# Column-wise substitution in the 16x16 blocks, and key products kept without their strengths, in a hybrid DeltaNet layer

## The chip, the cores and the metric

The kernel runs on one core of one Trainium2 chip. The metric is the device time of one execution in microseconds (us), lower is better. The engines are named as in the profile: PE (TensorE, with PEld for its weight loads), DVE (VectorE), ACT (ScalarE), POOL (GpSimd) and SP (SyncE, which here only starts transfers).

## The reference, cut to what matters

One layer works on 2048 latent tokens and 256 context tokens of width 1024. Branch A is a gated delta rule with 8 heads of 128 columns, run in both directions over chunks; the output of both directions is added, normalised, gated and projected. The part that the change touches is the inside of one chunk:

```python
m = jnp.where(tri_strict, jnp.einsum('bhncd,bhnsd->bhncs', k_beta, k) * decay, 0.0)
t_inv = lax.linalg.triangular_solve(eye + m, jnp.broadcast_to(eye, m.shape), left_side=True, lower=True)
u = jnp.einsum('bhncs,bhnsv->bhncv', t_inv, v_beta)
w = jnp.einsum('bhncs,bhnsd->bhncd', t_inv, k_beta * jnp.exp(g_cum)[..., None])
qk = jnp.einsum('bhncd,bhnsd->bhncs', q, k) * decay
def step(s, xs):
    v_new = u_i - jnp.einsum('bhck,bhkv->bhcv', w_i, s)
    o = jnp.einsum('bhck,bhkv->bhcv', q_dec_i, s) + jnp.einsum('bhcs,bhsv->bhcv', qk_i, v_new)
    s = s * d_i[..., None, None] + jnp.einsum('bhck,bhcv->bhkv', k_dec_i, v_new)
```

So each chunk needs the products of its keys with its keys (and with its queries), scaled by a decay and by a strength per key, and the inverse of a triangular matrix made from the first. The result need not be computed in chunks of 64; the kernel takes chunks of 128.

## The kernel before, in words

The kernel has three stages. The first computes the input projections (to about 1.85 ms of the trace). The second, called the window here, runs the delta rule. The third is the output projection with the final normalisation.

The window is a list of 36 **visits**: 18 chunks of 128 tokens (two of the context, sixteen of the latent tokens), each visited once in each direction, the two directions taking turns. A loop over i works on four visits at a time: v0 = visit i is in its state update (`st_ks`, `st_v`, `st_o`, `st_u`), v1 in the later steps of its inverse (`inv_w16` to `inv_d64`), v2 in its query products (`gram` with QK), v3 in its loads, its decays (`visit_decay`), its key products (`gram` with N) and the inverse of its 16x16 blocks (`inv_base`). Between them the loop puts a fixed number of **fillers**, single 512-column matmuls of the other projections (L1249, L1251, L1253), 24 a visit while i is under 25. PE's instructions run in the order in which the loop writes them. The order on DVE, ACT, POOL and SP is fixed when the kernel is built, by a scheduler; each of these engines then takes its list strictly in order.

A chunk is met twice, once in each direction. At the first meeting (a **fresh** visit; 16 of the 32 latent visits, all of them ahead of the others) `gram` computes the key products and stores them in DRAM (`kkd`, `kqd`) for the other direction. At the second meeting (an **again** visit) it loads them and multiplies them by that direction's decay (L151, L152).

The steps of a visit that the texts below speak of, with their lines in the kernel before:

- L137: ACT makes exp(gcb) for the queries (`qd`); POOL multiplies it by the queries (L138). DVE may overwrite `gcb` only after L137.
- L140: DVE, 8 times, difference of cumulated decays, with the mask. L142: ACT, exp of the result, so `gcb` now holds the decays of all 8 heads.
- L158: PE, key products, into two PSUM banks of 4 heads each. L163: ACT copies a bank to `zat`. L164: POOL multiplies the copy by the other direction's strengths. L165: SP stores it.
- L167: DVE, one instruction a head, products times strength (`cj`) times decay, gives N (and QK).
- L177, L180, L181, L182: ACT, then DVE, cut the 16x16 diagonal blocks out of N into `n16`.
- L191 to L193: the loop of 15 steps that inverts the blocks: a shuffle that spreads one row of R over its block, a multiplication, an addition. R is 128 x 8 heads x 16 columns.
- L196, L198: ACT spreads R to `r32`, DVE transposes it. L210 to L226: the step from 16 to 32. L247 to L267: from 32 to 64, ending in `r64t`.
- L278: PE, first product of the last step, needs `r64t`. L281: ACT copies it to `w64`. L288: PE, second product. L289: ACT puts it in R.
- L300, L302: PE and DVE, state times keys. L309, L312: new values and their copy. L320, L321: outputs. L328, L333: state update. L1287, L1288: ACT copies the output of a fresh visit, SP stores it.
- L118: POOL scales the keys of a later update (`kt`).

Of the kernel before, what the change touches and what calls it, by code (L numbers as in the profile page):

```python
# [7 lines left out]
F32 = mybir.dt.float32  # L8
# [24 lines left out]
def bc(ap, n):  # L33

    return ap.to_broadcast([ap.shape[0], ap.shape[1], n])


class Kern:
# [81 lines left out]
    def visit_decay(self, v):  # L120
# [21 lines left out]
        nc.scalar.activation(out=gcb, in_=gcb, func=AF.Exp)  # L142
        v["cj"] = cj

    def gram(self, v, name, rhs):
# [8 lines left out]
        for g in range(2):  # L154
# [4 lines left out]
            if v["latent"]:  # L159

                kc = self.g1.tile([P, 4, P], F32, name="zat", bufs=2)
                co = self.cc[:, v["n"], 8 - 8 * v["d"]:16 - 8 * v["d"]]
                nc.scalar.copy(out=kc, in_=kk)  # L163
                nc.gpsimd.tensor_tensor(out=kc, in0=kc, in1=bc(co[:, hs].unsqueeze(2), P), op=ALU.mult)  # L164
                nc.sync.dma_start(keep[:, hs], kc)  # L165
            for h in range(4 * g, 4 * g + 4):
                nc.vector.scalar_tensor_tensor(out=N[:, h, :], in0=kk[:, h - 4 * g, :], scalar=v["cj"][:, h:h + 1],  # L167
                                               in1=v["gcb"][:, h, :], op0=ALU.mult, op1=ALU.mult)


    def inv_base(self, v):
# [13 lines left out]
        nc.gpsimd.tensor_copy(out=R, in_=rows(self.i16))  # L185
        rb = g2.tile([P, H, 16], F32, name="rb")
        for i in (range(15, 0, -1) if d == 0 else range(0, 15)):
            c0, c1 = (i, 16) if d == 0 else (0, i + 1)
            w = c1 - c0
            rbv = rb.rearrange("p h c -> p (h c)")[:, 0:H * w].rearrange("p (h c) -> p h c", c=w)  # L190
            nc.vector.stream_shuffle(rbv, R[:, :, c0:c1], [i] * 16 + [16 + i] * 16)  # L191
            nc.vector.tensor_tensor(out=rbv, in0=rbv, in1=bc(n16[:, :, i:i + 1], w), op=ALU.mult)  # L192
            nc.vector.tensor_tensor(out=R[:, :, c0:c1], in0=R[:, :, c0:c1], in1=rbv, op=ALU.add)  # L193
        v["r32"] = r32 = g2.tile([P, H, 32], F32, name="r32")
# [974 lines left out]
    def window(self, es, settle):  # L1169
# [105 lines left out]
        def o_cb(n, again):  # L1275
# [7 lines left out]
            def cb(g, po):  # L1283
                hs = slice(4 * g, 4 * g + 4)
                ot = self.g1.tile([P, 4, P], F32, name="ot", bufs=3)
                if not again:
                    nc.scalar.copy(out=ot, in_=po)  # L1287
                    nc.sync.dma_start(self.o_d[n][:, hs], ot)  # L1288
                else:
                    nc.vector.tensor_tensor(out=ot, in0=po, in1=op[g], op=ALU.add)  # L1290
                    late.append((n, hs, ot))
# [354 lines left out]
```

## Time and profile before

| | us |
|---|---|
| median of 3 runs | 3217.88 |
| lowest and highest | 3211.53 and 3222.15 |
| the profiled execution | 3213.67 |
| its span in the trace | 3211.9 |
| granted PE clock, mean over the span | 0.965 of full speed |

The profiled execution is one run with a trace; its own time is 1.8 us more than the span that the trace covers, and it lies 4.2 us below the median of the three runs. All sums below are made against it. The trace has a row for each instruction with its start and its duration; neighbouring instructions of one engine overlap a little, so the distance from start to start is what an instruction costs its engine when nothing holds it up.

### The profile page before, as it was taken

What the parts mean: (1) busy time and instruction counts of PE and PEld (TensorE: products, weight loads), DVE (VectorE), ACT (ScalarE), POOL (GpSimd) and SP (SyncE); (2) the same over time, 40 slices, a digit from 0 to 9 for tenths busy, and PEclk for the clock granted to TensorE, in tenths of its full rate; (3) what the DMA queues carried; (4) which work ended last, traced back from release to release, by engine and by line L of the source; (5) the groups of instructions that cost most, each with busy time, mean ns of one, the idle gap of its engine ahead of it and who ended that gap; (6) DMA issues with size and microseconds to landing.
All of it is one profiled execution on the core that took longest, in us unless ns stands there. A gap on an engine that the chain in (4) does not pass through costs nothing.

```text
span 3211.9 us, 60563 instructions
## 1 busy us (share of the span) xinstructions
PE 2935.4 (91%) x22089; PEld 2411.4 (75%) x22089; DVE 2222.2 (69%) x5843; ACT 1512.2 (47%) x3405; POOL 1467.2 (46%) x1080
## 2 busy tenths in 40 slices
PE   7899899999998999999999988898999889896997
PEld 4678668888887777788878767788887777784776
DVE  7756746566656575566652268999999988866399
ACT  4564554333445646333344335555656656652121
POOL 3543547766567555566656402333322132315264
PEclk9999999999999999999999989999999889998999
DMA  5533773323565433222233387667677777787742
GB/s 211 143 110 90 231 221 112 102 79 122 175 195 173 126 89 97 58 88 79 79 124 109 117 283 253 218 235 254 212 264 272 261 237 264 247 268 248 238 152 102
DMA packets 405384, 557.26 MB, mean 173 GB/s; under 512 B 28245, under 2 KB 278614, under 8 KB 404061
## 3 DMA queue, kind: packets, MB, share of 16 engines
q1 hardware_dynamic: 395982, 545.94, 52.6%
q10 hardware_dynamic: 9102, 7.45, 0.7%
q8 instruction: 173, 2.83, 0.4%
q14 instruction: 127, 1.03, 0.1%
HBM read 391.66 MB, written 161.64 MB: 172 GB/s over the span
## 4 chain that ended last, share of the span: by engine, by line
PE 47%; DVE 26%; issue 7%; DMA 6%; ACT 6%; POOL 4%; SPq 1%; DVEq 0%; ACTq 0%; POOLq 0%
PE pd L763 12%; PE pd L764 12%; PE pd L765 12%; DVE R L193 3%; DVE rb L192 3%; POOL al L347 2%; DVE gcb L140 2%; DVE rb L191 2%; DVE t L1008 1%; DMA gcb<-gcd 1%; POOL s L749 1%; PE pf L1253 1%; ACT n L177 1%; PE pf L1249 1%; DVE t L1010 1%
## 5 line engine op out<-in xcount | busy, mean ns | idle before, releaser
L763 PE MATMUL pd<-bh,ah 128*128 128x512 f32 x2240 | 890.5, 398 | 10.4 <-ACT u L783 5.8
L765 PE MATMUL pd<-bh,al 128*128 128x512 f32 x2240 | 877.7, 392 | 0.0
L764 PE MATMUL pd<-bl,ah 128*128 128x512 f32 x2240 | 877.0, 392 | 0.0
L347 POOL TENSOR_TENSOR al<-s,ah 128x512 fp32r<-128x512 f32 x348 | 478.9, 1380 | 471.9 <-ACT ah L346 459.9
L347 POOL TENSOR_TENSOR al<-raw,ah 128x512 fp32r<-128x512 f32 x260 | 372.0, 1435 | 321.7 <-ACT ah L346 296.0
L763 PEld LDWEIGHTS pd<-bh,ah 128*128 128x128 f32 x2240 | 423.9, 189 | 98.9 <-issue 6.6
L765 PEld LDWEIGHTS pd<-bh,al 128*128 128x128 f32 x2240 | 423.4, 189 | 90.7 <-POOL al L347 0.4
L764 PEld LDWEIGHTS pd<-bl,ah 128*128 128x128 f32 x2240 | 424.3, 189 | 85.4
L346 ACT CAST ah<-s 128x512 fp32r<-128x512 f32 x352 | 214.6, 618 | 299.7 <-PE pd L764 265.8
L346 ACT CAST ah<-raw 128x512 fp32r<-128x512 f32 x264 | 162.4, 616 | 263.5 <-PE pd L764 166.7
L749 DVE TENSOR_TENSOR s<-s,raw 128x512 f32<-128x512 f32 x80 | 107.1, 1338 | 220.5 <-POOL s L749 216.3
L1249 PE MATMUL pf<-ah,wh 128*128 128x512 f32 x512 | 213.0, 417 | 43.1 <-DMA wh<-w_ahd 20.9
L1253 PE MATMUL pf<-ah,wl 128*128 128x512 f32 x512 | 219.3, 429 | 5.1 <-DMA wl<-w_ald 5.1
L1251 PE MATMUL pf<-al,wh 128*128 128x512 f32 x512 | 213.1, 416 | 2.1 <-POOL al L347 1.3
L138 POOL TENSOR_TENSOR qd<-qd,qT 128x1024 f32<-128x1024 f32 x32 | 76.5, 2391 | 256.9 <-ACT qd L137 242.4
L192 DVE TENSOR_TENSOR rb<-rb,n 128x8 f32<-128x8 f32 (+6 forms) x540 | 170.2, 316 | 4.8
L193 DVE TENSOR_TENSOR R<-R,rb 128x8 f32<-128x8 f32 (+6 forms) x540 | 157.4, 293 | 6.0
L1249 PEld LDWEIGHTS pf<-ah,wh 128*128 128x128 f32 x512 | 101.5, 198 | 65.8 <-issue 32.6
L118 POOL TENSOR_TENSOR kt<-kt,kd 128x1024 f32<-128x1024 f32 x36 | 70.2, 1950 | 154.7 <-DMA kt<-kd 108.9
L1025 ACT ACTIVATE t<-t 128x512 f32<-128x512 f32 (+1 forms) x112 | 67.2, 600 | 144.4 <-DVE t L1010 144.3
L140 DVE SCALAR_TENSOR_TENSOR gcb<-gcb,gc,mask 128x128 f32<-128x128 f32 x288 | 127.6, 449 | 4.8 <-ACT qd L137 2.7
L1253 PEld LDWEIGHTS pf<-ah,wl 128*128 128x128 f32 x512 | 101.2, 198 | 29.8 <-DMA wl<-w_ald 9.1
(353 smaller groups left out, 5982.1 us busy)
## 6 DMA issues: line engine op xcount, KB each, us to landing
raw<-in_w_in SPq DMA_DIRECT2D x160, 512.0 KB
kT<-kTd SPq DMA_DIRECT2D x36, 512.0 KB
gcb<-gcd SPq DMA_DIRECT2D x36, 512.0 KB
kt<-kd SPq DMA_DIRECT2D x36, 512.0 KB
vh<-vd SPq DMA_DIRECT2D x36, 512.0 KB
wh<-w_bhd SPq DMA_DIRECT2D x32, 512.0 KB
wl<-w_bld SPq DMA_DIRECT2D x32, 512.0 KB
qT<-qTd SPq DMA_DIRECT2D x32, 512.0 KB
```

The costliest lines, as they stand in the source:

```text
L140: nc.vector.scalar_tensor_tensor(out=gcb[:, h, :], in0=gcb[:, h, :], scalar=gcT[:, h:h + 1], in1=self.mask[d], op0=ALU.subtract, op1=ALU.min)
L192: nc.vector.tensor_tensor(out=rbv, in0=rbv, in1=bc(n16[:, :, i:i + 1], w), op=ALU.mult)
L193: nc.vector.tensor_tensor(out=R[:, :, c0:c1], in0=R[:, :, c0:c1], in1=rbv, op=ALU.add)
L346: self.nc.scalar.copy(out=hi, in_=src)
L347: (eng or self.nc.gpsimd).tensor_tensor(out=lo, in0=src, in1=hi.bitcast(F32), op=ALU.subtract)
L749: eng.tensor_tensor(out=o, in0=a, in1=b, op=op)
L763: mm(ps, hi[:, k, :], bh, start=(first and k == 0), stop=False, skip_group_check=not first)
L764: mm(ps, hi[:, k, :], bl, start=False, stop=False, skip_group_check=not first)
L765: mm(ps, lo[:, k, :], bh, start=False, stop=(last and k == 3), skip_group_check=not first)
L1249: mm(ps, wh[:, k, :], ah, start=(k == 0), stop=False)
L1251: mm(ps, wh[:, k, :], al, start=False, stop=False)
L1253: mm(ps, wl[:, k, :], ah, start=False, stop=(k == KT - 1))
```

## The change

1. The 16x16 blocks are inverted by columns instead of rows. Each step now spreads a row of the constant `n16` (not of R, which the loop itself changes) and multiplies it by a column of R. The shuffle of the next step stands between the multiplication and the addition of this step. The number of shuffles, multiplications and additions and their widths are as before.
2. DVE multiplies the decays `gcb` by the strengths in one instruction of 1024 columns a visit, in all 36 visits. The key products then need only one factor, so one DVE instruction of 512 columns takes a whole bank where there were four of 128.
3. The stored key products are no longer multiplied by POOL; ACT copies them and issues their store itself. ACT also issues the store of the outputs of fresh visits.

```diff
@@ visit_decay
         nc.scalar.activation(out=gcb, in_=gcb, func=AF.Exp)
-        v["cj"] = cj
+        nc.vector.tensor_tensor(out=gcb, in0=gcb, in1=bc(cj.unsqueeze(2), P), op=ALU.mult)
@@ gram
             if v["latent"]:
                 kc = self.g1.tile([P, 4, P], F32, name="zat", bufs=2)
-                co = self.cc[:, v["n"], 8 - 8 * v["d"]:16 - 8 * v["d"]]
                 nc.scalar.copy(out=kc, in_=kk)
-                nc.gpsimd.tensor_tensor(out=kc, in0=kc, in1=bc(co[:, hs].unsqueeze(2), P), op=ALU.mult)
-                nc.sync.dma_start(keep[:, hs], kc)
-            for h in range(4 * g, 4 * g + 4):
-                nc.vector.scalar_tensor_tensor(out=N[:, h, :], in0=kk[:, h - 4 * g, :], scalar=v["cj"][:, h:h + 1],
-                                               in1=v["gcb"][:, h, :], op0=ALU.mult, op1=ALU.mult)
+                nc.scalar.dma_start(keep[:, hs], kc)
+            nc.vector.tensor_tensor(out=N[:, hs], in0=kk, in1=v["gcb"][:, hs], op=ALU.mult)
@@ inv_base
-        rb = g2.tile([P, H, 16], F32, name="rb")
-        for i in (range(15, 0, -1) if d == 0 else range(0, 15)):
-            c0, c1 = (i, 16) if d == 0 else (0, i + 1)
-            w = c1 - c0
-            rbv = rb.rearrange("p h c -> p (h c)")[:, 0:H * w].rearrange("p (h c) -> p h c", c=w)
-            nc.vector.stream_shuffle(rbv, R[:, :, c0:c1], [i] * 16 + [16 + i] * 16)
-            nc.vector.tensor_tensor(out=rbv, in0=rbv, in1=bc(n16[:, :, i:i + 1], w), op=ALU.mult)
-            nc.vector.tensor_tensor(out=R[:, :, c0:c1], in0=R[:, :, c0:c1], in1=rbv, op=ALU.add)
+        order = list(range(0, 15) if d == 0 else range(15, 0, -1))
+        left = lambda j: slice(j + 1, 16) if d == 0 else slice(0, j)
+
+        def row(j):
+            c = left(j)
+            w = c.stop - c.start
+            t = g2.tile([P, H * 15], F32, name="rb", bufs=3)[:, 0:H * w].rearrange("p (h c) -> p h c", c=w)
+            nc.vector.stream_shuffle(t, n16[:, :, c], [j] * 16 + [16 + j] * 16)
+            return t
+
+        nxt = row(order[0])
+        for i, j in enumerate(order):
+            t, c = nxt, left(j)
+            nc.vector.tensor_tensor(out=t, in0=t, in1=bc(R[:, :, j:j + 1], c.stop - c.start), op=ALU.mult)
+            if i < 14:
+                nxt = row(order[i + 1])
+            nc.vector.tensor_tensor(out=R[:, :, c], in0=R[:, :, c], in1=t, op=ALU.add)
@@ o_cb, output of a fresh visit
-                    nc.sync.dma_start(self.o_d[n][:, hs], ot)
+                    nc.scalar.dma_start(self.o_d[n][:, hs], ot)
```

The lines after the loop move by four (L196 becomes L200, L281 becomes L285 and so on). PE's list has the same 11078 rows in the same order. The other engines' lists are new, since the scheduler made them again. Three places matter. In the rows, a name after `waits` is an engine or a transfer whose signal the instruction needs first.

First place: DVE in the middle of the loop of a fresh visit, before. The rows of the loop are L191 to L193; `S` is the state, `r_21123` belongs to the next size of the inverse.

```order
L226 STREAM_TRANSPOSE r32t<-r_21123 128x256 [waits DVE_49]
L192 TENSOR_TENSOR rb<-rb,n_21474 128x40 [waits DVE_49]
L193 TENSOR_TENSOR R_21478<-R_21478,rb 128x8x5 [waits DVE_49]
L191 STREAM_SHUFFLE rb<-R_21478 128x48 [waits DVE_49]
L192 TENSOR_TENSOR rb<-rb,n_21474 128x48 [waits DVE_49]
L193 TENSOR_TENSOR R_21478<-R_21478,rb 128x8x6 [waits DVE_49]
L191 STREAM_SHUFFLE rb<-R_21478 128x56 [waits DVE_49]
```

The same place in the changed kernel, where the widths fall instead of rising:

```order
L230 STREAM_TRANSPOSE r32t<-r_20754 128x256
L194 TENSOR_TENSOR rb<-rb,R_21094 128x56 [waits DVE_49]
L188 STREAM_SHUFFLE rb<-n_21090 128x40
L197 TENSOR_TENSOR R_21094<-R_21094,rb 128x8x7 [waits DVE_49]
L194 TENSOR_TENSOR rb<-rb,R_21094 128x48 [waits DVE_49]
L188 STREAM_SHUFFLE rb<-n_21090 128x32
L197 TENSOR_TENSOR R_21094<-R_21094,rb 128x8x6 [waits DVE_49]
```

Before, each of the three instructions waits for the one ahead of it; now the shuffle waits for none, and two instructions of three wait.

Second place: ACT from the decays' exponential (L142) to the blocks' copy (L177) of a fresh visit, before. `zat` is the copy of the key products, `w_21820` (now `w_21845`) is `w64`.

```order
L267 ACTIVATE r64t<-pinv 32x8x32 [waits PE_49,Activation_49]
L271 ACTIVATE R<-r_21666,m64l 128x8x64 [waits Activation_49]
L281 COPY w_21820<-pinv 64x512 [waits PE_49]
L271 ACTIVATE R<-r_21666,m64h 128x8x64
L131 ACTIVATE kd_22078<-t_22075 128x8 [waits DVE_49]
L142 ACTIVATE gcb<-gcb 128x1024 [waits DVE_49]
L289 ACTIVATE R<-pinv 64x8x64 [waits PE_49,Activation_49]
L163 COPY zat<-gram 128x512 [waits DMAHW0_49,PE_49,Pool_49]
L196 ACTIVATE r_21526<-R_21478,m16l 128x8x16 [waits DVE_49]
L196 ACTIVATE r_21526<-R_21478,m16h 128x8x16
L163 COPY zat<-gram 128x512 [waits DMAHW1_49,PE_49,Pool_49]
```

The same stretch now, from the exponential for the queries (L137) on:

```order
L137 ACTIVATE qd<-gcb 128x1024 [waits PE_49]
L200 ACTIVATE r_21558<-R_21496,m16l 128x8x16 [waits DVE_49]
L200 ACTIVATE r_21558<-R_21496,m16h 128x8x16
L1291 COPY ot<-pst 128x512 [waits DMAHW6_49,PE_49]
L269 ACTIVATE r_21690<-pinv 32x8x32 [waits PE_49]
L1292 DMA od_163<-ot 128x512 [waits DMAHW7_49,Activation_49]
L269 ACTIVATE r_21690<-pinv 32x8x32
L271 ACTIVATE r64t<-pinv 32x8x32 [waits PE_49]
L142 ACTIVATE gcb<-gcb 128x1024 [waits DVE_49]
L285 COPY w_21845<-pinv 64x512 [waits PE_49]
```

Three things moved: the copy to `w64` (L281, now L285) stands behind the decays' exponential instead of ahead of it; the spreading of R (L196, now L200) stands ahead of `r64t` instead of behind it; and stores stand in ACT's list.

Third place: DVE from the end of the loop to the blocks of the next visit, in the changed kernel (L143 is the new multiplication, L163 the key products, L176 the old L181, L306 the old L302, L337 the old L333):

```order
L197 TENSOR_TENSOR R_21094<-R_21094,rb 128x8 [waits DVE_49]
L1196 SCALAR_TENSOR_TENSOR gt<-gt,pf 128x512 [waits DMAHW3_49,PE_49]
L140 SCALAR_TENSOR_TENSOR gcb<-gcb,gc,mask_288 128x128 [waits Activation_49]
L202 STREAM_TRANSPOSE r32t<-r_21156 128x256 [waits Activation_49]
L140 SCALAR_TENSOR_TENSOR gcb<-gcb,gc,mask_288 128x128 x7
L337 SCALAR_TENSOR_TENSOR S_15793<-S_15793,d_20086,pst 128x128 [waits PE_49]
L337 SCALAR_TENSOR_TENSOR S_15793<-S_15793,d_20086,pst 128x128 x3
L143 TENSOR_TENSOR gcb<-gcb,cc 128x1024 [waits Activation_49]
L163 TENSOR_TENSOR N<-gram,gcb 128x512 [waits DVE_49,Activation_49]
L163 TENSOR_TENSOR N<-gram,gcb 128x512 [waits Activation_49]
L306 SCALAR_TENSOR_TENSOR vh<-pst,ngam,vh 128x128 [waits PE_49]
```

Before, the L140 rows stood between the steps of the loop, and six to eight L302 rows stood between the key products and L181; now the L140 rows follow the loop, and two to four of the L306 rows stand ahead of L176, the others inside the loop.

## Rows read from the trace of the kernel before

**Rows 1.** The page's busy time by engine (us, share of the span, instructions).

```profile
PE 2935.4 (91%) x22089; PEld 2411.4 (75%) x22089; DVE 2222.2 (69%) x5843; ACT 1512.2 (47%) x3405; POOL 1467.2 (46%) x1080
```

**Rows 2.** Windows: 13 fresh, 13 again visits (length, busy us by engine, PEclk, DMA, GB/s).

```profile
2020.10:2367.40 347.30, 319.70 (x4877) 285.63 (x4876) 321.26 (x1418) 203.88 (x429) 110.05 (x90) 0.99 0.69 234
2417.50:2788.10 370.60, 317.47 (x4611) 273.69 (x4610) 333.39 (x1402) 232.57 (x647) 95.15 (x63) 0.91 0.75 257
```

**Rows 3.** Waits of DVE, then of PE, 2020 to 2368 (us in total, times, longest).

```profile
DVE r32t L198 <- ACT r L196: 6.8, 6, 1.8
DVE n L181 <- ACT n L180: 6.3, 10, 0.8
...
PE pinv L278 <- ACT r64t L267: 9.5, 11, 1.6
```

**Rows 4.** DVE's instructions in order of time, a fresh visit (start us, us).

```profile
2206.77 0.17 DVE L192 TENSOR_TENSOR rb<-rb,n 128x24 f32<-128x24 f32 x1
2206.86 0.34 DVE L167 SCALAR_TENSOR_TENSOR QK<-gram,cc,gcb 128x128 f32<-128x128 f32 x1
2207.12 0.17 DVE L193 TENSOR_TENSOR R<-R,rb 128x24 f32<-128x24 f32 x1
...
2209.72 0.21 DVE L192 TENSOR_TENSOR rb<-rb,n 128x48 f32<-128x48 f32 x1
2209.97 0.21 DVE L193 TENSOR_TENSOR R<-R,rb 128x48 f32<-128x48 f32 x1
```

**Rows 5.** DVE groups by form (count, then busy us, mean ns).

```profile
L152 DVE TENSOR_TENSOR QK<-QK,gcb 128x1024 f32<-128x1024 f32 x16 | 19.5, 1218 | 1.3 <-DMA QK<-kqd 1.2
L1290 DVE TENSOR_TENSOR ot<-pst,op 128x512 f32<-128x512 f32 x32 | 21.9, 684 | 13.5 <-issue 6.3 <-PE pst L321 3.6 <-PE gram L1417 1.9
```

**Rows 6.** The narrowest loop steps, by form, 2020 to 2368.

```profile
L192 DVE TENSOR_TENSOR rb<-rb,n 128x8 f32<-128x8 f32 x13 | 7.1, 547 | 0.0
L193 DVE TENSOR_TENSOR R<-R,rb 128x8 f32<-128x8 f32 x13 | 6.2, 480 | 0.2
L193 DVE TENSOR_TENSOR R<-R,rb 128x16 f32<-128x16 f32 x13 | 6.0, 465 | 0.0
```

**Rows 7.** POOL and DVE side by side in one visit, in order of time.

```profile
2203.28 2.04 POOL L164 TENSOR_TENSOR zat<-zat,cc 128x512 f32<-128x512 f32 x2 [3.17 <-ACT zat L163]
2213.90 2.36 POOL L138 TENSOR_TENSOR qd<-qd,qT 128x1024 f32<-128x1024 f32 x1 [8.59 <-ACT qd L137]
...
2203.48 0.87 DVE L192 TENSOR_TENSOR rb<-rb,n 128x8 f32<-128x8 f32 x1
2214.21 2.16 DVE L192 TENSOR_TENSOR rb<-rb,n 128x88 f32<-128x88 f32 x1
```

**Rows 8.** ACT in order of time, from L137 on, and L281 and L142 of that visit.

```profile
2264.96 1.06 ACT L137 ACTIVATE qd<-gcb 128x1024 f32<-128x1024 f32 x1 [1.00 <-PE pst L320]
2267.31 0.37 ACT L267 ACTIVATE r64t<-pinv 32x256 f32<-32x256 f32 x1
2268.91 0.58 ACT L281 COPY w<-pinv 64x512 f32<-64x512 f32 x1 [0.48 <-PE pinv L278]
2272.86 1.06 ACT L142 ACTIVATE gcb<-gcb 128x1024 f32<-128x1024 f32 x1 [2.52 <-DVE gcb L140]
```

**Rows 9.** PE in order of time, 2215 to 2265: last step, key products, state, outputs.

```profile
2215.54 1.14 PE L278 MATMUL pinv<-r64t,N 64*64 64x64 f32 x16 [0.17 <-ACT r64t L267]
2218.87 1.14 PE L288 MATMUL pinv<-r,w 64*64 64x64 f32 x16
2223.90 1.95 PE L300 MATMUL pst<-S,kT 128*128 128x128 f32 x16
...
2251.89 1.95 PE L300 MATMUL pst<-S,kT 128*128 128x128 f32 x16
```

**Rows 10.** ACT issues a store straight behind its own instruction (stage before the window).

```profile
1834.60 0.72 ACT L602 ACTIVATE z<-z,biasT 128x512 f32<-128x512 f32 x1 [8.26 <-DVE z L791]
1835.35 0.38 ACTq L605 DMA_DIRECT2D zad<-z  x1
```

## The prediction, made before the changed kernel ran

> **What bounds the kernel now.** By busy time PE leads with 91% of the span against DVE's 69% [rows 1]. That average covers three stages; only the window is changed, so I read busy time by stretch. In thirteen fresh visits PE is busy 319.7 us of 347.3, but DVE 321.3 (92%), and in thirteen again visits DVE 333.4 of 370.6 against PE's 317.5 [rows 2]. One fresh visit takes 347.3/13 = 26.7 us, an again visit 28.5. The waits then say who holds whom. DVE waits for r32 6.8 us and for n16 6.3 us in thirteen visits, about 0.5 us a visit each, while PE waits 9.5 us for r64t alone [rows 3]. So in the window DVE hardly ever runs out of work: its list sets the length of a visit, and PE follows through ACT, which makes what PE reads out of what DVE made.
>
> PE's own chain is the next limit. In order of time, its last step of the inverse starts at 2215.54 and its state products at 2223.90, 8.4 us later; from the state products at 2251.89 [rows 9] to the end of the outputs (which releases L137 at 2264.96 [rows 8]) it is 13.1 us. ACT then needs 1.06 us for L137 and finishes r64t at 2267.68, 2.7 us after the outputs [rows 8]. Together 8.4 + 13.1 + 2.7 = 24.2 us: under 26.7, so PE has 2.5 us a visit in hand. A gain of DVE is paid out only down to this chain, and the chain itself is changed.
>
> **The change part by part: DVE.** Three prices first. A 128-column key product costs DVE 2207.12 - 2206.86 = 0.26 us from start to start although its row shows 0.34, since the next instruction starts 0.08 before it ends [rows 4]. With the same 0.08 off, a 512-column product out of PSUM costs 0.68 - 0.08 = 0.60 us and a 1024-column one in SBUF 1.22 - 0.08 = 1.14 [rows 5]; the trace has neither with exactly the new operands, so 0.60 to 0.68 and 1.14 to 1.22 are the bounds.
>
> *Products.* A fresh visit now has 16 of the short ones (N and QK), 4.2 us; afterwards four of 512 columns and the new multiplication, 2.4 + 1.14 = 3.5 us: -0.6 us. Again visits lose nothing and get +1.14 us.
>
> *Loop.* A step of 24 columns next to foreign work costs 0.09 us to the next start (2206.77 to 2206.86), but in a bare stretch an instruction of 48 columns that needs the one ahead costs 0.25 (2209.72 to 2209.97) [rows 4]. So a bare step costs 0.75 now, and in the new order, where the shuffle fits inside the multiplication's 0.25, it costs 0.50. Four or five of the fifteen steps stand bare in DVE's list; the others already have foreign instructions between. That is about -1.1 us in every visit. It cannot be under -15 x 0.25 = -3.8, nor over 0 (the same instructions in number and width).
>
> The Trainium skill ("VectorE: DVE Perf Modes", section Rules for kernel authors) speaks against this term: a drain follows each instruction of a chain regardless, so one should cut the number of instructions, not the semaphores between them. By that rule the loop term is 0 instead of -1.1. The trace here does not agree: 0.09 beside 0.25 us.
>
> *POOL.* A multiplication on POOL holds up DVE's instructions with two inputs in SBUF: while L138 runs from 2213.90 to 2216.26, a loop step that starts at 2214.21 takes 2.16 us. During L164 (from 2203.28) a step of 8 columns takes 0.87 [rows 7]. The three narrow forms that meet L164 take 7.1 + 6.2 + 6.0 = 19.3 us in 39 instructions [rows 6]; at the 0.17 of an undisturbed 24-column step [rows 4] it would be 6.6. L164 thus costs 12.7/13 = 1.0 us a fresh visit, which goes with it. L138's stall of about 2 us stays and only falls on other instructions.
>
> The Trainium skill ("SBUF — State Buffer", section Who interferes with whom) lets such an instruction contend with a POOL instruction that reads SBUF, and its section SBUF: two separate sides calls the read interface that the two engines share an exclusive lock, held for the whole instruction. The rows agree; by that the new 1024-column multiplication can be held up too, and products out of PSUM cannot.
>
> DVE alone: a fresh visit 26.7 - 0.6 - 1.1 - 1.0 = 24.0 us. An again visit +1.14 - 1.1 = 0.
>
> **ACT and PE.** ACT starts a store 0.03 us after its own instruction and spends 0.38 on it [rows 10]: 0.41 us for each of the six of a fresh visit, 2.5 us. ACT is busy only 203.9 of 347.3 us there [rows 2], so this costs nothing by itself; what counts is what stands behind a store. SP and POOL only lose work. The second place of the lists shows it: behind L137 now come both halves of the spreading of R (some 0.35 us each, as L267's rows [rows 8]), a copy that stood there before, and one store, ahead of r64t. r64t is ready 2.7 + 0.7 + 0.4 = 3.8 us after the outputs instead of 2.7, and PE's chain grows to 8.4 + 13.1 + 3.8 = 25.3 us.
>
> One wait is new. The decays' exponential stands ahead of the copy to w64. Call X the end of the outputs. L137 ends at X + 1.1; POOL's L138 then runs 2.36 us, to X + 3.5. The eight L140 now follow the loop, have two inputs in SBUF, and so finish 8 x 0.26 = 2.1 us later, at X + 5.6. The exponential takes 1.06 and the copy 0.58 [rows 8]; with some 0.3 of hand-overs w64 is ready at X + 7.6. PE wants it 3.3 us (2215.54 to 2218.87 [rows 9]) after the start of its last step, so at X + 3.8 + 3.3 = X + 7.1. PE stands 0.5 us: 25.8. Last, the wait for n16 (0.5 us now) loses four to six covering products of 0.26; I add 0.4 (bounds 0 and 1.0), since other DVE work is late too. A fresh visit: 26.2 us, -0.5, though DVE alone would do 24.0.
>
> **Sum.** 16 fresh visits x -0.5 = -8; the 16 again visits and four of the context 0. The profiled execution takes 3213.67 us, 4.2 below the median of 3217.88; 3213.7 - 8 = 3206. A measurement of this kernel can tell some 0.3% (9.7 us) from no change, so faster is under 3208.2 and slower over 3227.5. The forecast is only just on the fast side.
>
> **The rivals.** *DVE's relief is paid in full.* If the list of ACT slips without harm (w64 not late), fresh visits fall to PE's 25.3 us or, where r64t keeps its old 2.7, to DVE's 24.0: -1.4 to -2.7 a visit, 3191 to 3170. For it speaks that DVE is busy 92% [rows 2]; against it, that two of PE's operands move back in ACT's list.
>
> *No change.* The gain of 0.5 a visit is the difference of terms of 2 to 3 us. If PE's new standing for w64 is 1.0 instead of 0.5, the visit is again 26.7: 3214. The total then shows nothing, with DVE's idle time up by 2.7 us a visit.
>
> *Slower: PE waits on DVE's decays.* One mechanism: w64 waits for the decays' exponential, and this for the last L140. Each us by which DVE ends the L140 later than X + 5.6 is a us of PE's time, and with them the state update that the next visit of this direction needs. It decides at 26.7 - 26.2 = 0.5 us, an end at X + 6.1. If DVE comes to them 1.7 us late (a 2-us stall of the loop by L138 ahead of them instead of beside them), a fresh visit takes 27.9, +1.2 x 16 = +19; again visits have the same order of ACT, and with half of them 1 us longer it is +8 more: 3241. For it speaks that all eight now follow the loop; against it, that DVE has 2.7 us less to do before.
>
> *The loop gains nothing.* If an instruction costs 0.25 in the loop whether or not it needs the one ahead, again visits pay the new multiplication: 16 x 1.14 = +18. Fresh visits keep their -8 at best, 0 at worst: 3224 to 3232. Against it speak the 0.09 us of [rows 4]. The rule of the Trainium skill named above ("VectorE: DVE Perf Modes") would give this case.
>
> **How the numbers follow.** The forecast (3198 to 3214) has 0.36; the full relief 0.18; no change 0.19; slower by w64 0.20; no gain in the loop 0.07. Predicted is the likeliest, 3206. The range leaves out the far ends of the full relief and of the slower case: 3172 to 3240. Faster: three quarters of the forecast and the whole of the relief, 0.27 + 0.18 = 0.45; same: 0.09 + 0.19 + 0.02 = 0.30; slower: 0.20 + 0.05 = 0.25.
>
> **What would show it.** Fresh visits: DVE's busy share under 90%, no loop step of 8 columns over 0.3 us, bare loop steps at 0.5, products at 0.60. PE should wait for w64 (L285's copy), by 0.4 us or more a visit, and for r64t. Again visits: 28.5 as now. The prediction is wrong if PE's waits for w64 are absent (then faster) or over 1 us a visit (then no gain), or if the new multiplication is held by POOL's L118 or L138 in again visits, where up to 2 us each would decide.

## The result and the profile after

The changed kernel takes 3254.43 us (median of four runs, 3242.34 to 3256.41) against 3220.02 for the kernel before in the same series: a ratio of 1.0101, 95% interval 1.0079 to 1.0124. It is slower by 1%, on the other side of the forecast of 3206 and outside the range. The profiled execution took 3242.34 us, the fastest of the four and 28.7 more than that of before; the comparisons below are made with it, so that they explain 28.7 of the 34.4 us by which the medians differ. One execution of e1 below took 8029.81 us; its ratio leaves it out.

The busy times of the page, to be held against [rows 1]:

```profile
PE 2950.9 (91%) x22089; PEld 2420.2 (75%) x22089; DVE 2172.1 (67%) x5663; ACT 1516.4 (47%) x3405; POOL 1404.8 (43%) x1016
```

DVE and POOL have less to do, and the kernel is slower. Next the windows: thirteen fresh visits (from one product of new values to that of the thirteenth visit after it), then thirteen again visits, columns as in [rows 2]:

```profile
2012.00:2384.00 372.00, 334.06 (x4905) 297.35 (x4907) 285.45 (x1278) 207.34 (x429) 60.66 (x39) 0.94 0.68 221
2438.40:2814.00 375.60, 320.58 (x4627) 273.39 (x4626) 337.98 (x1428) 233.62 (x649) 98.33 (x64) 0.93 0.75 252
```

A fresh visit takes 372.0/13 = 28.6 us instead of 26.7, an again visit 28.9 instead of 28.5. In fresh visits DVE is busy 285.5/13 = 22.0 us, 77% of the time instead of 92%: 2.7 us less than the 24.7 of [rows 2], as forecast. PE is busy 25.7 us a visit instead of 24.6, for the same instructions, at a granted clock of 0.94 instead of 0.99.

The waits of PE, then of DVE, then of ACT in the same thirteen fresh visits (total us, times, longest), against [rows 3]:

```profile
PE pinv L282 <- ACT r64t L271: 32.2, 13, 4.7
PE pinv L292 <- ACT w L285: 3.5, 5, 0.9
...
DVE N L163 <- ACT zat L161: 36.8, 24, 5.2
DVE t L128 <- DMA gcb<-gcd: 22.6, 13, 2.8
...
ACT kd L131 <- DVE rb L194: 25.7, 11, 3.5
```

PE now stands 2.5 us a visit for r64t (0.7 before) and only 0.3 for w64. DVE stands 2.8 us a visit for a copy that ACT makes of PE's product, that is, for PE itself, and 1.7 us for a load of gcb, for which it hardly waited before. ACT's wait is put down to a loop step of DVE, since that comes last by the profile; the instruction, L131, needs the result of L128 and L129, and so that load.

One visit shows how these hang together (rows of DVE, SP, ACT and PE; L131 is an exponential of 8 columns for the keys of the next visit):

```profile
2220.05 0.68 DVE L163 TENSOR_TENSOR QK<-gram,gcb 128x512 f32<-128x512 f32 x1
2219.88 0.32 SPq L117 DMA_DIRECT2D vh<-vd  x1
2220.76 0.32 SPq L104 DMA_DIRECT2D gcb<-gcd  x1
2226.93 0.17 DVE L128 SCALAR_TENSOR_TENSOR t<-gc,gcb 128x8 f32<-128x8 f32 x1 [1.98 <-DMA gcb<-gcd]
2227.41 0.21 ACT L131 ACTIVATE kd<-t 128x8 f32<-128x8 f32 x1 [2.77 <-DVE rb L194]
2227.52 1.04 ACT L137 ACTIVATE qd<-gcb 128x1024 f32<-128x1024 f32 x1
2227.93 0.17 DVE L197 TENSOR_TENSOR R<-R,rb 128x8 f32<-128x8 f32 x1
2228.47 0.39 ACT L200 ACTIVATE r<-R,m16l 128x128 f32<-128x128 f32 x1
2230.56 0.38 ACT L271 ACTIVATE r64t<-pinv 32x256 f32<-32x256 f32 x1
2225.43 0.39 PE L325 MATMUL pst<-v,QK 128*128 128x128 f32 x2
2227.18 1.05 PE L332 MATMUL pst<-v,kt 128*128 128x128 f32 x8
2230.99 1.64 PE L282 MATMUL pinv<-r64t,N 64*64 64x64 f32 x16 [2.75 <-ACT r64t L271]
```

Read it as a chain. The last QK product on DVE ends at 2220.73 and frees gcb; SP starts the load for the next visit at 2220.76, with a load of vh just ahead of it. The data are there at about 2226.9, when DVE's L128 stops waiting. ACT's list holds L131 ahead of L137 and of r64t, and L131 needs that gcb, through L128 and L129. L137 does not: counted through the trace, it reads the gcb loaded a visit earlier, and its list gives it PE alone to wait for; it only stands behind L131. DVE's list holds L128 ahead of the last steps of the loop, so that R, which L200 spreads, is ready no earlier either (2228.10). The outputs had ended at 2225.82, but r64t is ready only at 2230.94, 5.1 us later and not 3.8. PE has stood for 2.75 us by then. L131 stands ahead of L137 in 11 of these 13 visits.

### The profile page after: what moved, and what is told of

Its sections match the earlier page's. It is cut to its first block, busy times and chain, and to the rows that moved or that the text cites. A ratio compares the mean times of both kernels' runs of the same rounds, so it can differ in the third digit from the quotient of the medians.

```text
span 3240.6 us, 60302 instructions
## 1 busy us (share of the span) xinstructions
PE 2950.9 (91%) x22089; PEld 2420.2 (75%) x22089; DVE 2172.1 (67%) x5663; ACT 1516.4 (47%) x3405; POOL 1404.8 (43%) x1016
## 4 chain that ended last, share of the span: by engine, by line
PE 47%; DVE 22%; DMA 8%; issue 7%; ACT 7%; POOL 4%; SPq 1%; ACTq 0%; DVEq 0%; POOLq 0%
PE pd L767 12%; PE pd L769 12%; PE pd L768 12%; DMA gcb<-gcd 3%; DVE gcb L140 3%; POOL al L351 2%; DVE rb L188 2%; ACT n L172 1%; DVE R L197 1%; DVE t L1012 1%; POOL s L753 1%; PE pf L1257 1%; DVE vh L306 1%; PE pf L1253 1%; PE pf L1255 1%
## 5 line engine op out<-in xcount | busy, mean ns | idle before, releaser
L138 POOL TENSOR_TENSOR qd<-qd,qT 128x1024 f32<-128x1024 f32 x32 | 75.3, 2352 | 417.4 <-ACT qd L137 392.7
L118 POOL TENSOR_TENSOR kt<-kt,kd 128x1024 f32<-128x1024 f32 x36 | 75.1, 2087 | 181.8 <-DMA kt<-kd 164.5
L140 DVE SCALAR_TENSOR_TENSOR gcb<-gcb,gc,mask 128x128 f32<-128x128 f32 x288 | 144.7, 555 | 12.6 <-ACT qd L137 11.4
L197 DVE TENSOR_TENSOR R<-R,rb 128x120 f32<-128x120 f32 (+4 forms) x540 | 128.6, 238 | 1.2
L194 DVE TENSOR_TENSOR rb<-rb,R 128x120 f32<-128x120 f32 (+4 forms) x540 | 123.1, 228 | 3.3 <-DVE rb L188 0.3
L1257 PEld LDWEIGHTS pf<-ah,wl 128*128 128x128 f32 x512 | 103.7, 203 | 28.6 <-DMA wl<-w_ald 6.8
```

Of the source, the lines that this page charges most:

```text
L140: nc.vector.scalar_tensor_tensor(out=gcb[:, h, :], in0=gcb[:, h, :], scalar=gcT[:, h:h + 1], in1=self.mask[d], op0=ALU.subtract, op1=ALU.min)
L194: nc.vector.tensor_tensor(out=t, in0=t, in1=bc(R[:, :, j:j + 1], c.stop - c.start), op=ALU.mult)
L197: nc.vector.tensor_tensor(out=R[:, :, c], in0=R[:, :, c], in1=t, op=ALU.add)
L1257: mm(ps, wl[:, k, :], ah, start=False, stop=(k == KT - 1))
```

## The experiments

The figure "fresh" is the mean distance between the starts of thirteen successive products of new values in the traces: 26.8 us before, 28.6 in the changed kernel. Each ratio is to the kernel before on the same chip.

| run | median, us | ratio (95% interval) | fresh, us |
|---|---|---|---|
| e1 columns only | 3253.28 | 1.0125 (1.0108 to 1.0142) | 28.6 |
| e2 changed, old loop | 3217.13 | 1.0013 (0.9997 to 1.003) | 26.7 |
| e3 changed, stores on SP | 3249.96 | 1.0122 (1.0095 to 1.0148) | 28.4 |
| e4 stores only | 3224.36 | 1.0036 (1.0024 to 1.0048) | 27.7 |
| e5 changed, products first | 3248.75 | 1.0112 (1.0092 to 1.0131) | 28.8 |
| e6 changed, narrow steps first | 3258.67 | 1.0143 (1.0126 to 1.016) | 29.7 |
| e7 rows, wide steps first | 3211.36 | 0.9993 (0.998 to 1.0006) | 26.8 |
| e8 changed, third gcb | 3225.68 | 1.0038 (1.0023 to 1.0053) | 27.4 |
| e9 columns only, written late | 3198.29 | 0.9943 (0.9925 to 0.9961) | 25.8 |
| e10 changed, loop late | 3250.39 | 1.0108 (1.0075 to 1.0141) | 28.0 |
| e11 changed, loop late, stores on SP | 3190.27 | 0.9920 (0.9894 to 0.9945) | 24.9 |
| e12 products only | 3202.88 | 0.9961 (0.9944 to 0.9978) | 25.9 |
| e13 as e10, w64 first | 3211.76 | 0.9989 (0.9973 to 1.0006) | 26.6 |
| e14 as e10, outputs stored by SP | 3206.53 | 0.9976 (0.9963 to 0.9989) | 26.2 |
| e15 as e10, products stored by SP | 3243.35 | 1.0083 (1.0062 to 1.0104) | 27.5 |
| e16 changed, decays written late | 3256.35 | 1.0126 (1.0098 to 1.0153) | 28.6 |

**One part at a time: e1, e2, e3, e4, e12.** The edits are the parts of the change's own diff: e1 and e4 put one part into the kernel before, e2 and e3 take one out of the changed kernel.

```diff
# e2: loop by rows back in the changed kernel; e1: the loop by columns in the kernel before
# e3: in the changed kernel
-                nc.scalar.dma_start(keep[:, hs], kc)
+                nc.sync.dma_start(keep[:, hs], kc)
-                    nc.scalar.dma_start(self.o_d[n][:, hs], ot)
+                    nc.sync.dma_start(self.o_d[n][:, hs], ot)
# e4: the reverse of e3 in the kernel before
```

> The kernel before with the column-wise loop alone. Theory G (the changed kernel is slow because the next visit's gcb lands late, behind a load of vh that now goes first, and ACT's list waits for it ahead of r64t): here gcb is loaded ahead of vh as before in nearly all fresh visits, so no loss; the loop gives -1.1 us of DVE a visit, 3185 to 3212 us. Theory A (the loss is ACT's list itself: R is spread ahead of r64t, 0.7 us, and the decays' exponential stands ahead of the copy to w64): R is spread ahead of r64t here too, but that is within PE's 2.5 us in hand; 3205 to 3220. Theory L (the column loop itself gains nothing): 3217 to 3223.

> The changed kernel with the old loop by rows (unscaled products and ACT's stores stay). One store stands ahead of r64t, R behind it, the exponential behind w64, and gcb is loaded ahead of vh. Theory G: DVE waits for gcb under 0.3 us a visit, fresh visits 26 us or less, 3195 to 3225 in all (again visits pay 1.14 us each). Theory A: the one store costs 0.4 us of ACT, 3215 to 3230. If ACT's stores are the cause by themselves: as slow as the changed kernel, 3245 to 3255.

> The changed kernel with all its stores issued by SP again (column loop and unscaled products stay). The exponential is behind w64 again and no store stands ahead of r64t, but vh is loaded ahead of gcb in most fresh visits and the small decays kd stand ahead of L137 on ACT. Theory G: gcb still lands 5.5 to 6.5 us after its issue, DVE waits 1 to 2 us a fresh visit for it, and the time stays at 3240 to 3255. Theory A: stores and exponential are out of the way, so it falls to 3205 to 3225.

> The kernel before with ACT issuing the stores of products and outputs, nothing else (old loop, POOL's multiplication). vh goes ahead of gcb in most fresh visits, one store stands ahead of r64t, R behind it, the exponential behind w64. Theory G: slower, 3228 to 3245, with DVE waiting for gcb about 1 us a fresh visit. Theory A: one store of 0.4 us within PE's slack, no change, 3215 to 3225.

The column loop alone costs 1.25%, no less than the whole change, and without it the rest of the change costs nothing that can be told (e2). Taking the stores off ACT brings nothing back (e3); ACT's stores alone cost 0.36% (e4). I had not expected this of e1: none of the theories gave 3253. Theory G does not explain it, since PE hardly waits for r64t there. Its premise for e1 was wrong as well: in the trace of e1 the load of vh is issued ahead of that of gcb (at 2193.62 and 2197.79). What PE waits for in e1:

```profile
PE pinv L256 <- DVE r32t L235: 28.5, 12, 3.9
PE pinv L287 <- ACT r64t L276: 5.9, 8, 0.9
```

It is r32t of the next size of the inverse, an instruction of DVE. So I counted in DVE's list how many of the loop's 15 steps (by their shuffles) stand ahead of the instructions that others wait for:

| | ahead of r32t (next size) | ahead of the last QK product | ahead of the first L140 |
|---|---|---|---|
| before | 5 | 4 | 11 or 12 |
| changed | 10 | 8 | 15 |
| e1 | 13 | 12 | 15 |
| e3 | 11 | 9 | 15 |
| e2 | 4 | 4 | 13 |

From this came theory O: the loop by columns always has an instruction that is ready (the next shuffle needs only a constant), so that the scheduler puts more of the loop ahead of instructions that became ready a little later, on which PE and the load of gcb depend; afterwards DVE has nothing to do. By this theory the loop's own instructions are no slower.

**What of the order: e5 to e8.** e5 raises products and r32t; e6 and e7 turn the widths around (their loops do not compute the inverse; kinds, counts and widths of the instructions are kept); e8 gives gcb a third buffer.

```diff
# e5, also around nc.scalar.copy(out=kc, in_=kk) and around the products that make N and QK
+        with self.tc.high_priority(200):
             nc.vector.scalar_tensor_tensor(out=r32[:, :, cs], in0=dp[:, :, cs], scalar=self.m16[d], ...)
             nc.vector.transpose(self.fl(r32t), self.fl(r32))
# e6
-        order = list(range(0, 15) if d == 0 else range(15, 0, -1))
+        order = list(range(14, -1, -1) if d == 0 else range(1, 16))
+        col = slice(15, 16) if d == 0 else slice(0, 1)
-            nc.vector.tensor_tensor(out=t, in0=t, in1=bc(R[:, :, j:j + 1], c.stop - c.start), op=ALU.mult)
+            nc.vector.tensor_tensor(out=t, in0=t, in1=bc(R[:, :, col], c.stop - c.start), op=ALU.mult)
# e7, in the kernel before
-        for i in (range(15, 0, -1) if d == 0 else range(0, 15)):
+        for i in (range(1, 16) if d == 0 else range(14, -1, -1)):
-            nc.vector.tensor_tensor(out=R[:, :, c0:c1], in0=R[:, :, c0:c1], in1=rbv, op=ALU.add)
+            nc.vector.tensor_tensor(out=R[:, :, c0:c1], in0=rbv, in1=rbv, op=ALU.subtract)
# e8
-        self.gb = self.pool(es, "gb", 2)
+        self.gb = self.pool(es, "gb", 3)
```

> The changed kernel with the key products (ACT's copy and DVE's multiplication) and the two instructions that end in r32t of the next size raised in the scheduler's priority, nothing else. In DVE's list 5 loop steps instead of 8 then stand ahead of the last QK product (which frees gcb for its next load) and 5 instead of 10 ahead of r32t; the decays' exponential stays ahead of the copy to w64 and one store ahead of r64t. Theory O (the loss is the order on DVE: the column loop has a ready instruction at every moment and its widest steps first, so it crowds out what PE and the load of gcb wait for): 3195 to 3222, r32t 5 us after n16 or less. Theory A (exponential and stores in ACT's list): 3235 to 3255.

> The changed kernel with the loop's widths rising from 8 to 120 columns instead of falling; each step multiplies by the one column that every step writes, so that it still needs the step ahead (the loop does not compute the inverse). Count, kinds and widths of the instructions are those of the changed kernel. 8 loop steps, the narrow ones, stand ahead of r32t. Theory O with widths as the main part: 3205 to 3225. Theory O with the loop's readiness (the number of steps ahead) as the main part: 3225 to 3245. If the column form costs by itself: 3245 to 3255.

> The kernel before with the loop's widths falling from 120 to 8 instead of rising; the last instruction of a step writes a difference of rb with itself, so the loop does not compute the inverse, with the same kinds, counts and widths. 5 loop steps, now wide ones, stand ahead of r32t, as before. If widths are the main part: 3225 to 3245. If readiness is: 3208 to 3222, as before.

> The changed kernel with a third buffer for gcb, so that its load no longer waits for the last QK product; DVE's list keeps 8 to 10 loop steps ahead of QK and r32t. If the late gcb is how the late products reach PE: DVE's wait for gcb goes (1.7 us a fresh visit now), PE's wait for r64t falls from 2.5 to about 1.4 us, 3212 to 3230. If r32t itself is what PE waits for in the end: 3240 to 3255.

e7 says that the widths alone are not the cause: in the loop by rows, wide steps first cost nothing. In e8 some 20 of the 34 us are gone (1.0038 against 1.0101), but not as I had expected: the load of gcb still lands late, and DVE still waits for it (17.0 us). What changed are places in the lists. In 11 of 13 visits L131 now stands behind r64t on ACT, and L128 behind the loop on DVE. The waits of PE in e8, then one such visit (PE, ACT, DVE, ACT):

```profile
PE pinv L282 <- ACT r64t L271: 16.6, 13, 3.6
PE pinv L292 <- ACT w L285: 13.9, 11, 1.6
...
2215.30 0.39 PE L325 MATMUL pst<-v,QK 128*128 128x128 f32 x2
2215.50 1.06 ACT L137 ACTIVATE qd<-gcb 128x1024 f32<-128x1024 f32 x1 [1.00 <-PE pst L324]
2217.99 1.04 DVE L128 SCALAR_TENSOR_TENSOR t<-gc,gcb 128x8 f32<-128x8 f32 x1 [2.19 <-DMA gcb<-gcd]
2218.56 0.37 ACT L271 ACTIVATE r64t<-pinv 32x256 f32<-32x256 f32 x1
2224.64 0.19 ACT L131 ACTIVATE kd<-t 128x8 f32<-128x8 f32 x1
```

gcb lands 2.3 us after the outputs, later than in the visit of the changed kernel above, and r64t is ready 3.2 us after them instead of 5.1. So the late load as such is not the loss; what stands behind it in the lists is. Part of the gain goes to w64 at once: PE's wait for it rises from 3.5 to 13.9 us. No run moves L131 alone.

e5 came out at the time that theory A gave, not theory O. It lets r32t and QK through, and the time does not change. The waits of PE in e5 and of ACT in e6 show what became of it:

```profile
PE pinv L295 <- ACT w L288: 11.9, 13, 0.9
PE pst L316 <- DVE vh L309: 10.8, 24, 1.0
PE pinv L285 <- ACT r64t L274: 4.7, 13, 0.4
```

```profile
ACT r L201 <- DVE R L198: 29.0, 11, 3.5
```

In e5 the wait for r64t is nearly gone, but PE now waits for the products of state and keys (vh), which stand between the steps of the loop, and for w64. e6 was slower than any theory gave. ACT waits 29.0 us there for the end of the loop, with the spreading of R (L201), which its list holds ahead of r64t: I had counted that place at its own 0.7 us, not at the wait that it can bring. Why narrow steps first make the loop end so late is not settled.

**Only the place of the loop: e9, e10, e11.** The loop is cut off the function that makes n16 and called one iteration later, behind the decays; nothing else changes. e9 has it with the column loop alone, e10 with the whole change, e11 with the whole change and all stores on SP.

```diff
@@ inv_base is cut in two behind n16
+        v["n16"] = n16
+    def inv_loop(self, v):
         R = g2.tile([P, H, 16], F32, name="R16")
...
@@ the loop over the visits
                 if v3:
                     self.visit_decay(v3)
+                if v2:
+                    self.inv_loop(v2)
```

> Columns only (as in the run with the column loop alone), but the loop and what follows it in its step are written one iteration later, behind the decays of the next visit, so that the scheduler puts everything that PE waits for ahead of it: 2 loop steps instead of 13 stand ahead of r32t, 2 instead of 12 ahead of the last QK product, and 13 or 14 ahead of the first L140. Same instructions, same operands. Theory O (order on DVE): the whole loss of columns alone goes, 3190 to 3215. If the column form costs by itself (its operands, its waits): 3235 to 3255.

> The changed kernel with the loop written one iteration later: 3 steps instead of 10 ahead of r32t, 3 instead of 8 ahead of QK; vh's load is behind gcb's; one store ahead of r64t and the decays' exponential ahead of w64 stay as in the changed kernel, and all loop steps still stand ahead of the L140. Theory O: 3200 to 3222. Theory A (what stays in ACT's list, above all w64 behind the exponential): 3228 to 3250, with PE's wait for w64 at 0.8 us a visit or more.

> The run before (changed kernel, loop one iteration later) with all stores on SP: no store ahead of r64t, w64 ahead of the exponential, 2 loop steps ahead of r32t and QK. Theory O: 3190 to 3212, the best of all if the products' saving is real. Theory A: 3195 to 3215 too, so this one only tells whether anything is left that neither names: then 3225 or more.

> The kernel before with the unscaled products alone: decays multiplied by the strengths in one instruction, products of 512 columns, ACT's copy, no multiplication on POOL; stores on SP, the old loop. DVE has 1.6 us less in a fresh visit and 1.14 more in an again visit. Theory O: no order is disturbed, DVE's relief turns into waits or into at most -0.5 us a fresh visit: 3205 to 3222. If again visits pay the new multiplication in full: 3220 to 3232.

e1 and e9 have the same instructions, on PE in the same order, and differ only in the order on the other engines: 1.0125 against 0.9943. The place of the column loop was therefore the loss of e1, and written late it is a gain of 0.6% on the kernel before. How much of the 0.6% is the form and how much the place is not shown: the old loop by rows was not tried in the late place. The products alone (e12) gain 0.4%. Both together with the stores on SP (e11) are the fastest kernel of the study, at 0.9920. A window of some thirteen of its visits:

```profile
2020.00:2345.00 325.00, 316.52 (x4900) 283.59 (x4899) 292.62 (x1272) 204.26 (x430) 62.13 (x39) 1.00 0.76 253
```

The three longest waits of PE in e11, 2016 to 2370:

```profile
PE pst L329 <- ACT v L321: 4.5, 5, 1.4
PE pinv L287 <- ACT r64t L276: 3.6, 15, 0.3
PE pst L318 <- DVE vh L311: 2.1, 2, 1.5
```

PE is busy 97% of the stretch at full clock: here it is the bound. But e10, with the same loop and ACT's stores, is as slow as the changed kernel. The end of the outputs on PE, then POOL, DVE, ACT and PE in one of its visits:

```profile
2216.57 0.39 PE L330 MATMUL pst<-v,QK 128*128 128x128 f32 x2
2217.90 2.37 POOL L138 TENSOR_TENSOR qd<-qd,qT 128x1024 f32<-128x1024 f32 x1 [17.22 <-ACT qd L137]
2217.96 2.35 DVE L202 TENSOR_TENSOR R<-R,rb 128x32 f32<-128x32 f32 x1
2221.09 2.18 DVE L140 SCALAR_TENSOR_TENSOR gcb<-gcb,gc,mask 128x128 f32<-128x128 f32 x8
2223.31 1.06 ACT L142 ACTIVATE gcb<-gcb 128x1024 f32<-128x1024 f32 x1 [2.95 <-DVE gcb L140]
2224.97 0.58 ACT L290 COPY w<-pinv 64x512 f32<-64x512 f32 x1
2225.61 1.24 PE L297 MATMUL pinv<-r,w 64*64 64x64 f32 x16 [2.53 <-ACT w L290]
```

This is the prediction's slower rival, step by step: POOL's L138 holds up a loop step for 2.35 us, the eight L140 come behind it, ACT's exponential waits for them, the copy to w64 stands behind the exponential, and PE stands 2.53 us. The outputs end at 2216.96, which is X, and the L140 at 2223.27, X + 6.3: past the point of X + 6.1 that the prediction named. PE waits so in 7 of 13 visits of e10 (16.9 us).

**Which stores, and by time or by order: e13 to e16.** All are made from e10, but e16 from the changed kernel.

```diff
# e13
-        with self.tc.high_priority(100):
+        with self.tc.high_priority(400):
             nc.scalar.copy(out=v["w64"][p2], in_=wp[p2])
# e14: the outputs' store on nc.sync;  e15: the key products' store on nc.sync
# e16: L140, the exponential and the multiplication by cj become a function of their own
                 if v1:
                     self.inv_w64(v1)
+                if v3:
+                    self.visit_decay2(v3)
```

> The changed kernel with the loop one iteration later and all stores on ACT, as in e10, with one thing more: the copy to w64 has a higher priority, which puts it ahead of the decays' exponential in ACT's list in all fresh visits but one. Theory W (w64 behind the exponential, which waits for the L140 that POOL's L138 holds up): PE's wait for w64 falls from 1.3 us a visit to under 0.3, 3195 to 3218. Theory S (the stores cost by ACT's time): as e10, 3238 to 3256.

> As e10, but only the key products are stored by ACT (four stores a fresh visit), the outputs by SP. The exponential stands behind the copy to w64, no store ahead of r64t. Theory W: 3188 to 3212. Theory S: two thirds of the loss stays, 3225 to 3245.

> As e10, but only the outputs are stored by ACT (two stores a fresh visit), the key products by SP. The exponential stands ahead of the copy to w64 and one store ahead of r64t, as in e10. Theory W: 3230 to 3255. Theory S: a third of the loss, 3203 to 3220.

> The changed kernel, loop and stores as they are, with the second half of the decays (L140, exponential, multiplication by the strengths) written behind the step that makes w64, so that the copy to w64 stands ahead of the exponential. DVE's list keeps 10 loop steps ahead of r32t and vh's load stays ahead of gcb's. Theory O: PE waits for r64t (2.5 us a visit) and not for w64 (0.3 us), so little changes: 3238 to 3256. If w64 is the cause in the changed kernel too: 3205 to 3225.

Moving one copy of ACT (e13) takes 39 us off e10, with all stores still on ACT. e15, with only two stores a visit but the exponential ahead, is slow; e14, with four stores and the exponential behind, is fast. The waits of PE in e15, then one of PE and one of ACT in e13:

```profile
PE pinv L297 <- ACT w L290: 25.4, 13, 2.5
PE pinv L287 <- ACT r64t L276: 4.0, 13, 0.3
```

```profile
PE pinv L287 <- ACT r64t L276: 13.5, 12, 2.1
ACT kd L131 <- DVE t L129: 17.6, 7, 4.0
```

So the stores did most of their harm through the order that they bring. Some 16 to 21 us remain between e11 and e13 or e14, and the traces show where: in 7 of 14 visits of each, L131 stands ahead of L137 again and waits (17.6 us in e13, 15.1 in e14; 2.6 in e11, where it never stands there), and r64t then comes up to 5.7 us after the outputs instead of 2.5 to 2.7. In the changed kernel itself, putting the copy to w64 ahead of the exponential gains nothing (e16): there PE is already held by r64t.

## Why the prediction was wrong

**What bounds the kernel** held: DVE's list set the pace of fresh visits, with PE 2.5 us behind as the next limit. In e11, where DVE's relief is paid out, the visit falls to 24.9 us. The limit there is PE's own work, 24.3 us a visit; it was 319.7/13 = 24.6 in [rows 2], so that PE had 2.1 us in hand and not the 2.5 of the chain of 24.2.

**The prices of DVE held, but for one.** Instructions of DVE in order of time in the changed kernel: a product with what follows it, and a bare stretch of the loop.

```profile
2219.01 0.68 DVE L163 TENSOR_TENSOR QK<-gram,gcb 128x512 f32<-128x512 f32 x1
2219.62 0.23 DVE L194 TENSOR_TENSOR rb<-rb,R 128x80 f32<-128x80 f32 x1
...
2222.54 0.21 DVE L194 TENSOR_TENSOR rb<-rb,R 128x48 f32<-128x48 f32 x1
2223.02 0.20 DVE L194 TENSOR_TENSOR rb<-rb,R 128x40 f32<-128x40 f32 x1
```

Groups by form of the thirteen fresh visits (count, then busy us, mean ns): the narrowest step and the new multiplication.

```profile
L197 DVE TENSOR_TENSOR R<-R,rb 128x8 f32<-128x8 f32 x13 | 2.3, 174 | 0.4
L143 DVE TENSOR_TENSOR gcb<-gcb,cc 128x1024 f32<-128x1024 f32 x13 | 22.3, 1713 | 0.8 <-ACT gcb L142 0.2
```

A bare step takes 2223.02 - 2222.54 = 0.48 us (0.50 forecast), a product 0.61 (0.60), the narrowest step 0.17 instead of the 0.48 to 0.55 of [rows 6]. Only the new multiplication is dearer: its row is 1.71 us on average instead of 1.22, since POOL holds it up in six of the thirteen visits (last section). With that, the products' term comes to 4 x 0.61 + 1.63 = 4.1 us against 4.2, about -0.1 and not -0.6. That DVE's busy time fell by just the 2.7 us forecast is therefore partly luck: the loop and POOL gave more than their 2.1. The Trainium skill ("VectorE: DVE Perf Modes", section Rules for kernel authors) would have had the reordered loop cost what it did; the 0.48 does not agree with it.

**The step that failed** is the sentence that r64t is ready 3.8 us after the outputs ("r64t is ready 2.7 + 0.7 + 0.4 = 3.8 us after the outputs instead of 2.7"), and with it the chain of 25.3 us. It let L137 start when the outputs end and counted what ACT's instructions behind it take, not what ACT waits for ahead of it. The count was right: from the start of L137 to r64t it is 2230.94 - 2227.52 = 3.4 us in the visit shown, within the 3.8. The wait was put at nothing: L137 started 1.7 us after the outputs, behind L131 and the load that L131 needs, and r64t came 5.1 us after them. ACT stands so for 25.7 us in 11 of 13 fresh visits, and PE 2.5 us a visit. The list from which the prediction read ACT's order begins with L137, one row too late to show L131; in the list of before, L131 stands behind r64t. It did stand ahead of L137 in 5 of 14 fresh visits before, and there r64t came 4.0 us after the outputs, against 2.5 to 2.7 in the others; the prediction's 2.7 is one of these. The load itself was issued no later than before, measured against the outputs: 5.1 us ahead of their end here, 4.6 in a visit of before (issued at 2208.34, outputs ended at 2212.96). Nor did the prediction use what the first place of the lists shows, that r32t had moved behind more of the loop's steps (10 instead of 5), and QK with it; e1 and e9 show what that alone can cost. That the loop's term would be -1.1 us in every visit was right as a sum of DVE's work and wrong as a gain: where in the list the work stands was worth more (e1 against e9, 55 us by the medians).

A second term was left out altogether. Standing for long cost PE more than the wait: its clock fell (below), and it was busy 25.7 us a fresh visit instead of 24.6. In the visit shown PE is done with its other work at 2227.18 + 1.05 = 2228.23, 2.4 us after the outputs; by the forecast it would have stood 3.8 - 2.4 = 1.4 us for r64t, and it stood 2.5 on average. As a rough account, 26.2 + 1.1 (r64t) + 1.1 (clock) - 0.2 (w64) = 28.2 of the 28.6 us measured.

**The new wait for w64** was right as a mechanism and put in the wrong place: 3.5/13 = 0.3 us a visit in the changed kernel, where r64t hides it (e16), and 1.1, 1.3 and 2.0 us in e8, e10 and e15, where r64t came earlier. The slower rival's time of 3241 was the nearest, but by luck: the cause was not its own.

**ACT's stores** "cost nothing by themselves" was about right as to ACT's time (207 us busy of 372), but e4 shows that they are not free: 0.36%, by the other runs most likely through the lists that they change. **Again visits** went from 28.5 to 28.9 us, not to 28.5.

By parts: columns +1.25%, stores +0.36%, products -0.39%. Their sum, +1.2%, is close to the +1.0% of the whole; but with the loop late the stores cost 60 us (e10 against e11), so that parts do not simply add.

## What to carry to other kernels

When a scheduler fixes an engine's order, a chain that is broken up (so that it always has an instruction ready) also gets more of the engine ahead of work that others wait for; write it, or rank it, behind that work, and then measure. When pricing an instruction that now stands ahead of a critical one, ask what it waits for, not only how long it takes, and read the list from far enough ahead: here an exponential of 8 columns, whose result is needed only a visit later, held up what PE was waiting for. A gain in busy time on the bounding engine can be real and be lost entirely to order: the same instructions here took 1.25% more and 0.6% less than the kernel before.

## What the runs showed of the hardware

PE's granted clock fell with its long waits. In the changed kernel, fillers after the 2.75 us of standing took 0.63 us instead of 0.39, and the granted clock from 2231.0 to 2234.4 was 0.56 of full speed (last row, columns as in [rows 2]), so mostly the lower of the two levels; from 2234.9 on it was 1.00 again:

```profile
2226.95 0.39 PE L1255 MATMUL pf<-al,wh 128*128 128x512 f32 x1
...
2233.15 0.63 PE L1253 MATMUL pf<-ah,wh 128*128 128x512 f32 x1
2231.00:2234.40 3.40, 3.40 (x20) 2.93 (x21) 3.40 (x12) 1.04 (x1) 1.12 (x2) 0.56 0.40 158
```

Over fresh visits the clock was 0.94 of full speed (the two levels are 1.2 and 2.4 GHz), 0.99 before and 1.00 in e11, where PE hardly stood. In e5 PE stood as long in all as in the changed kernel (39 us against 37) but never over 1.1 us at a time, and its clock was 0.99.

POOL's multiplication of keys (L118) holds up the new 1024-column multiplication:

```profile
2233.56 1.90 POOL L118 TENSOR_TENSOR kt<-kt,kd 128x1024 f32<-128x1024 f32 x1 [2.28 <-DMA kt<-kd]
2234.45 2.09 DVE L143 TENSOR_TENSOR gcb<-gcb,cc 128x1024 f32<-128x1024 f32 x1
```

It takes 2.09 us there, against 1.22 where nothing runs on POOL, and ends 1.1 us after POOL does. The 512-column products out of PSUM are not held: in e11 two of them take 1.37 us together from 2025.76 on, while L118 runs from 2025.62 to 2027.52. The Trainium skill ("SBUF — State Buffer", section Who interferes with whom) says that an instruction with two inputs in SBUF contends with a POOL instruction that reads SBUF; the trace agrees.
